# Attention transposes one tile later, and key copies by DMA, in a fused attention and linear-attention block

## The chip, the cores and the metric

The kernel runs on one core of one Trainium2 chip. The metric is the device time of one execution in microseconds (us), the median over several runs. A core has five engines with queues of their own: PE (TensorE: matmuls, with the weight loads shown as PEld), DVE (VectorE), ACT (ScalarE), POOL (GpSimd) and SP (SyncE), which here issues nearly all DMAs. Each engine works through its own list of instructions in order, and waits on semaphores for the others.

## The reference

One encoder layer on 512 positions of width 2048, in float32:

```
h    = rms_norm(x) * (1 + scale) + shift          # scale, shift, gate from silu(c) @ w_cond + b_cond
proj = h @ w_in                                   # queries, keys, values, gates, GLA inputs
for each of 3 (window, dilation) patterns:        # 16 heads x 64
    s = q k^T / 8 + bias, masked;  p = exp(s - max) / sum;  o = p v
att  = the three o, merged with weights from their softmax denominators
a_out = att * silu(ag)
g_out = rms_norm(gla_fwd + gla_bwd) * gain * silu(gg)   # 4 heads, chunked gated linear attention
x    = x + gate * (concat(a_out, g_out) @ w_out);  return rms_norm(x) * final_gain
```

The kernel folds the three patterns into one softmax per head, with the multiplicity of a key in the bias row.

## The kernel before

**Precision.** Matmul operands are split into a high part (rounded to the fast float32 form, `F32R`) and a low part (the rest); `three` (L168 to L171) multiplies high by high, low by high and high by low into one PSUM tile.

**Stages.** A planned start (conditioning sums, norm, values and the first projections, tiles `sta` and `stb`) runs until about 193 us. Then come *units*: one unit is one projection of 512 columns over all 2048 inputs, 64 steps ("ticks") of three 512-wide matmuls each, into four PSUM tiles. The units are `qk2`, `qk4`, `qk6`, `gk`, `gv0`, `gv1`, `ag0`, `ag1`, `gg0`, `gg1` and the output's `o0` to `o3`. A unit's weights come in eight groups of 512 KB (`raw_...`, `fetch`), fetched some groups ahead through four buffers and split by ACT (L313) and DVE (L297).

**Side work.** `unit` takes a list of side items, each with a place between 0 and 1, and issues each between ticks. Attention is the side work of `qk2`, `qk4`, `qk6` and `gk`: four heads in each, four query tiles of 128 per head, so 16 tiles a unit. `attention` builds 40 items, spread over the unit by `ATT_AT`:

- *score* (s): two matmuls (L576, L577) into PSUM tile `s`; DVE adds the bias row `g` and takes the extreme (L580), ACT takes the exponential with its sum (L583), DVE the reciprocal (L584), POOL scales the tile `p` by it (L585). `p` is a buffer of pool `t2`.
- *turn* (t): four PE transposes of `p` (L597) into PSUM tile `t`; ACT copies the high part (L601), DVE makes the low part (L602), both into `pt`.
- *values* (o): for two query tiles at once eight matmuls (L611) into `o`, then ACT (L614) and DVE (L618) into `cat`.

The items go out in the order s(x), t(x-1), o(x-2), where o comes only behind odd tiles. The first two items are moved to the unit's places 0.14 and 0.15, the last one over the unit's end. PSUM tiles `s`, `t` and `o` share three buffers (`PA`); the projections have five (`PJ`), of which a unit uses four.

**Stacks.** `qk_evict` takes the queries and keys of a pair of heads out of PSUM (at the end of the planned start, and at the end of each of the three `qk` units, so that it runs beside the start of the next one). A head's own 64 rows are one half of a 128-row tile. `qs` holds the queries' high part in the own half and the low part in the other; `ks` holds the keys' high part in *both* halves, `kl` the keys' low part in both. ACT writes the two halves of `ks` (L548, L549), DVE the two of `kl` (L550, L551), all read from PSUM. All twelve stack tiles of a unit and the `p` tiles are buffers of `t2`, 15 of 2 KB per partition.

**Order.** PE's order is that of the program. On the other engines a scheduler orders the instructions; `urgent` raises the priority of side items. In the stage in question every DMA goes out on SP.

Of the kernel before, what the change touches and what calls it, by code (L numbers as in the profile page):

```python
# [10 lines left out]
F32 = mybir.dt.float32  # L11
F32R = mybir.dt.float32r
I32 = mybir.dt.int32
AF = mybir.ActivationFunctionType
ALU = mybir.AluOpType
# [118 lines left out]
def block_kernel(ctx: ExitStack, tc: tile.TileContext, a: dict):  # L134
    nc = tc.nc
# [1 line left out]
    hp = ctx.enter_context(tc.tile_pool(name="hp", bufs=2))  # L137
    wp = ctx.enter_context(tc.tile_pool(name="wp", bufs=3))
    b8 = ctx.enter_context(tc.tile_pool(name="b8", bufs=8))
    t2 = ctx.enter_context(tc.tile_pool(name="t2", bufs=15))  # L140
    gp = ctx.enter_context(tc.tile_pool(name="gp", bufs=2))
    sm = ctx.enter_context(tc.tile_pool(name="sm", bufs=4))
    pp = ctx.enter_context(tc.tile_pool(name="pp", bufs=4, space=PSUM))
# [3 lines left out]
    def T2(name, dt=F32, parts=P):  # L147
        return t2.tile([parts, 512], dt, tag="t2", name=name)

    def B8(name, shape, dt=F32):  # L150
        return b8.tile([P] + shape, dt, tag="b8", name=name)
# [4 lines left out]
    def PA(name):  # L156
        return pp.tile([P, 512], F32, tag="pa", bufs=3, name=name)

    mm = nc.tensor.matmul
    tt = nc.vector.tensor_tensor  # L160
    stt = nc.vector.scalar_tensor_tensor
    act = nc.scalar.activation
# [314 lines left out]
    n = len(chain) // 2  # L477
# [53 lines left out]
    def qk_evict(p, psq, psk):  # L531

        for j in range(2):
            own = slice(64 * j, 64 * j + 64)
            oth = slice(64 - 64 * j, 128 - 64 * j)
            qs = T2(f"qs{p}{j}", F32R)
            act(qs[own], psq[own, ::-1], AF.Copy, scale=-0.125)
            stt(qs[oth], psq[own, ::-1], -0.125, qs[own].bitcast(F32),  # L540
                op0=ALU.mult, op1=ALU.subtract)
            stacks[2 * p + j] = [qs, None, None, own]
        for j in range(2):
            own = slice(64 * j, 64 * j + 64)
            oth = slice(64 - 64 * j, 128 - 64 * j)
            ks = T2(f"ks{p}{j}", F32R)
            kl = T2(f"kl{p}{j}", F32R)
            act(ks[own], psk[own], AF.Copy)  # L548
            act(ks[oth], psk[own], AF.Copy)  # L549
            tt(kl[own], psk[own], ks[own].bitcast(F32), op=ALU.subtract)  # L550
            tt(kl[oth], psk[own], ks[own].bitcast(F32), op=ALU.subtract)  # L551
            stacks[2 * p + j][1:3] = ks, kl

    cat = [None] * 4
# [1 line left out]
    def attention(pairs):  # L556

        tiles = [(2 * p + j, i) for p in pairs for j in range(2) for i in range(4)]
        gt, pt, pr_ = {}, {}, {}
        heads = [2 * p + j for p in pairs for j in range(2)]  # L560

        def g_load(h):
            g = gp.tile([P, 896], F32, tag="g", name=f"g{h}")
            nc.sync.dma_start(g, bass.AP(grow.tensor, grow.offset + h * 1024, [[1, P], [1, 896]]))
            gt[h] = g

        def score(h, i):
            def go():
                if h % 8 == 0 and i == 0:
                    cat[h // 8] = B8(f"cat{h // 8}", [4, 512])  # L570
                if i == 1 and h != heads[-1]:
                    g_load(h + 1)
                qs, ks, kl, _ = stacks[h]
                q = slice(P * i, P * i + P)
                ps = PA(f"s{h}{i}")
                mm(ps, qs[:, q], ks, start=True, stop=False)  # L576
                mm(ps, qs[:, q], kl, start=False, stop=True)  # L577
                t = T2(f"p{h}{i}")
                st = sm.tile([P, 3], F32, tag="st", name=f"st{h}{i}", bufs=6)
                nc.vector.tensor_tensor_reduce(  # L580
                    out=t, in0=ps, in1=gt[h][:, P * i:P * i + 512], op0=ALU.add, op1=ALU.min,
                    scale=1.0, scalar=3e38, accum_out=st[:, 0:1])
                act(t, t, AF.Exp, bias=st[:, 0:1], scale=-1.0, accum_out=st[:, 1:2])  # L583
                nc.vector.reciprocal(st[:, 2:3], st[:, 1:2])  # L584
                nc.gpsimd.tensor_scalar(t, t, st[:, 2:3], 1.0, op0=ALU.mult, op1=ALU.mult)  # L585
                pr_[h, i] = t
            return go

        def turn(h, i):
            def go():  # L590
                half, ii = divmod(i, 2)
                if ii == 0:
                    pt[h, half] = B8(f"pt{h}{half}", [2, 4, 256], F32R)
                t = pr_.pop((h, i))
                pk = PA(f"t{h}{i}")
                for kt in range(4):
                    nc.tensor.transpose(pk[:, kt * P:kt * P + P], t[:, kt * P:kt * P + P], ident)  # L597
                hi = pt[h, half][:, 0, :, P * ii:P * ii + P]
                lo = pt[h, half][:, 1, :, P * ii:P * ii + P]
                src = pk.rearrange("p (k q) -> p k q", k=4)  # L600
                act(hi, src, AF.Copy)  # L601
                tt(lo, src, hi.bitcast(F32), op=ALU.subtract)  # L602
            return go

        def values(h, half):
            def go():
                t = pt.pop((h, half))
                po = PA(f"o{h}{half}")
                for kt in range(4):
                    for w in range(2):  # L610
                        mm(po[:, :256], vv[h // 4][:, kt, h % 4, :], t[:, w, kt, :],  # L611
                           start=kt == 0 and w == 0, stop=kt == 3 and w == 1)
                oh = sm.tile([64, 256], F32, tag="oh", name=f"oh{h}{half}", bufs=1)
                act(oh, po[64:128, :256], AF.Copy)  # L614
                own = stacks[h][3]
                p = h // 2
                dst = cat[p // 4][own, p % 4, 256 - 256 * half:512 - 256 * half]
                tt(dst[:, ::-1], po[0:64, :256], oh, op=ALU.add)  # L618
            return go

        items = []
        n = len(tiles)
        for x in range(n + 3):
            if x < n:
                items.append(score(*tiles[x]))
            if 1 <= x <= n:
                items.append(turn(*tiles[x - 1]))
            if 2 <= x <= n + 1 and tiles[x - 2][1] % 2 == 1:
                items.append(values(tiles[x - 2][0], tiles[x - 2][1] // 2))
        g_load(heads[0])  # L630
        start, span, move0, move1, move_last = ATT_AT
        at = [start + (q + 0.5) / len(items) * span for q in range(len(items))]
        at[0] -= move0
        at[1] -= move1
        at[-1] += move_last
        return list(zip(at, items))
# [263 lines left out]
    for p in range(2):  # L900
        qk_evict(p, psb["b", 4 + 2 * p], psb["b", 5 + 2 * p])
    for n, p in (("qk2", 0), ("qk4", 2), ("qk6", 4)):
        ps = unit(n, False, attention((p, p + 1)) + ([(0.05, shift_row)] + some_sums(n) if p == 4 else []))
        for q in range(2):
            qk_evict(p + 2 + q, ps[2 * q], ps[2 * q + 1])

    ps = unit("gk", False, attention((6, 7)) + some_sums("gk"))
    gla["k"] = B8("gkt", [4, 512])
    for i in range(4):
# [221 lines left out]
```

## Time and profile before

| | |
|---|---|
| median of 3 runs | 975.26 us (973.75 to 977.06) |
| the profiled execution | 973.38 us, its span 971.6 us |
| PE busy | 943.0 us (97% of the span) |
| DVE, ACT, POOL busy | 616.6 (63%), 441.0 (45%), 81.6 us (8%) |
| chain that ended last | PE 81%, DVE 8%, DMA 3%, ACT 3%, issue 3% |
| DMA moved | 159.56 MB |
| granted TensorE clock | 0.997 of full |

Engine shares are of the whole span; the four units with attention fill about 193 to 476 us of it. The ends of matmuls are modelled: back-to-back 512-wide matmuls are listed with 0.39 us each, but start 0.23 us apart.

### The profile page before, as it was taken

What the parts mean: (1) busy time and instruction counts of PE and PEld (TensorE: products, weight loads), DVE (VectorE), ACT (ScalarE), POOL (GpSimd) and SP (SyncE); (2) the same over time, 40 slices, a digit from 0 to 9 for tenths busy, and PEclk for the clock granted to TensorE, in tenths of its full rate; (3) what the DMA queues carried; (4) which work ended last, traced back from release to release, by engine and by line L of the source; (5) the groups of instructions that cost most, each with busy time, mean ns of one, the idle gap of its engine ahead of it and who ended that gap; (6) DMA issues with size and microseconds to landing.
All of it is one profiled execution on the core that took longest, in us unless ns stands there. A gap on an engine that the chain in (4) does not pass through costs nothing.

```text
span 971.6 us, 11885 instructions
## 1 busy us (share of the span) xinstructions
PE 943.0 (97%) x4464; PEld 775.7 (80%) x4464; DVE 616.6 (63%) x916; ACT 441.0 (45%) x735; POOL 81.6 (8%) x100
## 2 busy tenths in 40 slices
PE   8999999989999999999999999999999999999996
PEld 4888788878778777778777888888888888888884
DVE  7988999566665676775534647585885352546431
ACT  5443533655655645655413544363744151333222
POOL 0000000011111122012000000000010000202120
PEclk9999999999999999999999999999999999999998
DMA  9998687422222253332444334355465455244013
GB/s 333 414 411 347 238 302 258 133 85 96 92 84 82 85 193 105 126 128 84 146 152 166 121 109 152 130 176 171 139 228 176 152 175 193 87 148 156 22 50 124
DMA packets 42619, 159.56 MB, mean 164 GB/s; under 512 B 5217, under 2 KB 5505, under 8 KB 37825
## 3 DMA queue, kind: packets, MB, share of 16 engines
q1 hardware_dynamic: 42386, 158.48, 47.2%
q8 instruction: 35, 0.57, 0.2%
q10 hardware_dynamic: 176, 0.33, 0.1%
q14 instruction: 22, 0.18, 0.1%
HBM read 154.51 MB, written 4.28 MB: 163 GB/s over the span
## 4 chain that ended last, share of the span: by engine, by line
PE 81%; DVE 8%; DMA 3%; ACT 3%; issue 3%; POOL 1%; SPq 0%; ACTq 0%; DVEq 0%; POOLq 0%
PE ps_o L170 6%; PE ps_o L171 6%; PE ps_o L169 6%; PE sta L169 3%; PE sta L170 3%; PE sta L171 3%; PE stb L171 3%; PE stb L169 3%; PE stb L170 3%; PE ps_qk L169 3%; PE ps_gv L170 3%; PE ps_gv L171 3%; PE ps_gv L169 3%; PE ps_qk L171 3%; PE ps_qk L170 3%
## 5 line engine op out<-in xcount | busy, mean ns | idle before, releaser
L585 POOL TENSOR_SCALAR p<-p,st 128x512 f32<-128x512 f32 x64 | 46.1, 721 | 424.3 <-DVE st L584 407.8
L583 ACT ACTIVATE p<-p,st 128x512 f32<-128x512 f32 x64 | 46.2, 722 | 63.4 <-DVE st L580 63.4
L244 DVE CUSTOM_DVE_ANT_0 cb<-cb,sb,c_bcond 128x2048 f32<-128x2048 f32 (+1 forms) x32 | 73.4, 2294 | 0.0
L602 DVE TENSOR_TENSOR pt<-t,pt 128x512 fp32r<-128x512 f32 x64 | 44.1, 689 | 17.8 <-ACT pt L601 17.8
L597 PE MATMUL t<-c_ident,p 128*128 128x128 f32 x256 | 38.9, 275 | 10.6 <-POOL p L585 10.6
L597 PEld LDWEIGHTS t<-c_ident,p 128*128 128x128 f32 x256 | 30.9, 140 | 22.3 <-POOL p L585 15.4
L580 DVE CUSTOM_DVE_ANT_0 p<-s,g 128x512 f32<-128x512 f32 x64 | 43.6, 686 | 7.0 <-PE s L577 6.1
L601 ACT ACTIVATE pt<-t 128x512 fp32r<-128x512 f32 x64 | 37.8, 591 | 21.1 <-PE t L597 20.5
L244 DVE CUSTOM_DVE_ANT_0 rawg<-rawg,sb,gate 128x1024 f32<-128x1024 f32 x16 | 20.7, 1294 | 27.8 <-DMA rawg<-in_wg 27.8
L611 PEld LDWEIGHTS o<-pt,vv 128*128 128x128 f32 x256 | 34.2, 189 | 3.8 <-DVE pt L602 1.7
L244 DVE CUSTOM_DVE_ANT_0 rawg<-rawg,sb,c_bcond 128x1024 f32<-128x1024 f32 x16 | 20.5, 1283 | 25.2 <-DMA rawg<-in_wg 25.2
L611 PE MATMUL o<-pt,vv 128*128 128x256 f32 x256 | 35.9, 283 | 0.0
L1014 POOL TENSOR_TENSOR x<-x,fgain 128x512 f32<-128x512 f32 x12 | 20.0, 1675 | 183.8 <-ACT ysq L1012 183.8
L1012 ACT ACTIVATE ysq<-x 128x512 f32<-128x512 f32 x16 | 10.1, 632 | 47.1 <-DVE x L1010 44.8
L767 POOL TENSOR_SCALAR dc<-st,sc 128x256 f32<-128x256 f32 x16 | 10.5, 656 | 242.5 <-DVE st L764 237.6
L584 DVE RECIPROCAL st<-st 128x1 f32<-128x1 f32 x64 | 10.4, 162 | 31.3 <-ACT p L583 31.2
L1009 DVE TENSOR_TENSOR y<-ps_o,sb 128x512 f32<-128x512 f32 x16 | 10.9, 684 | 25.9 <-PE ps_o L171 25.9
L576 PE MATMUL s<-ks,qs 128*128 128x512 f32 x64 | 25.3, 395 | 0.2 <-DVE qs L540 0.2
L577 PE MATMUL s<-kl,qs 128*128 128x512 f32 x64 | 25.0, 391 | 0.0
L774 ACT ACTIVATE sq<-st,sc 128x256 f32<-128x256 f32 x24 | 12.2, 509 | 26.2 <-DVE st L769 13.8
L618 DVE TENSOR_TENSOR cat<-o,oh 64x256 f32<-64x256 f32 x32 | 13.3, 415 | 11.9 <-ACT oh L614 11.7
L614 ACT ACTIVATE oh<-o 64x256 f32<-64x256 f32 x32 | 12.2, 380 | 17.3 <-PE o L611 16.5
(1279 smaller groups left out, 2944.6 us busy)
## 6 DMA issues: line engine op xcount, KB each, us to landing
cb<-in_wm SPq DMA_DIRECT2D x31, 1024.0 KB, 7.5
rawg<-in_wg SPq DMA_DIRECT2D x32, 512.0 KB, 3.4
raw_o<-in_w_o SPq DMA_DIRECT2D x32, 512.0 KB, 3.4
raw_qk<-in_w_qk SPq DMA_DIRECT2D x24, 512.0 KB, 3.3
rawb<-in_w_sb SPq DMA_DIRECT2D x16, 512.0 KB, 4.3
rawv<-in_wv SPq DMA_DIRECT2D x16, 512.0 KB, 3.4
raw_gv<-in_w_gv SPq DMA_DIRECT2D x16, 512.0 KB, 3.4
raw_ag<-in_w_ag SPq DMA_DIRECT2D x16, 512.0 KB, 3.4
```

The costliest lines, as they stand in the source:

```text
L169: mm(ps, lh, rh, start=first, stop=False)
L170: mm(ps, ll, rh, start=False, stop=False)
L171: mm(ps, lh, rl, start=False, stop=last)
L244: nc.vector.tensor_tensor_reduce(out=w, in0=w, in1=with_, op0=ALU.mult, op1=ALU.add, scale=1.0, scalar=init, accum_out=dst)
L576: mm(ps, qs[:, q], ks, start=True, stop=False)
L580: nc.vector.tensor_tensor_reduce(out=t, in0=ps, in1=gt[h][:, P * i:P * i + 512], op0=ALU.add, op1=ALU.min, scale=1.0, scalar=3e38, accum_o ...
L583: act(t, t, AF.Exp, bias=st[:, 0:1], scale=-1.0, accum_out=st[:, 1:2])
L585: nc.gpsimd.tensor_scalar(t, t, st[:, 2:3], 1.0, op0=ALU.mult, op1=ALU.mult)
L597: nc.tensor.transpose(pk[:, kt * P:kt * P + P], t[:, kt * P:kt * P + P], ident)
L601: act(hi, src, AF.Copy)
L602: tt(lo, src, hi.bitcast(F32), op=ALU.subtract)
L611: mm(po[:, :256], vv[h // 4][:, kt, h % 4, :], t[:, w, kt, :], start=kt == 0 and w == 0, stop=kt == 3 and w == 1)
```

## The change

1. The items of an attention unit go out in the order s(x), t(x-2), o(x-3): the transposes of a tile's P stand two score tiles behind its score matmuls, not one. The number of items and their places in the unit stay.
2. The second halves of `ks` and `kl` are copied out of the first halves by two DMAs on SP, 64 partitions x 2 KB (128 KB) each, in place of an ACT and a DVE instruction that read PSUM.
3. Pool `t2` has 16 buffers instead of 15; the 2 KB per partition come from a scratch area of another kind of DMA, which the kernel does not use.

```diff
-    t2 = ctx.enter_context(tc.tile_pool(name="t2", bufs=15))
+    t2 = ctx.enter_context(tc.tile_pool(name="t2", bufs=16))
...
             act(ks[own], psk[own], AF.Copy)
-            act(ks[oth], psk[own], AF.Copy)
+            nc.sync.dma_start(ks[oth].bitcast(F32), ks[own].bitcast(F32))
             tt(kl[own], psk[own], ks[own].bitcast(F32), op=ALU.subtract)
-            tt(kl[oth], psk[own], ks[own].bitcast(F32), op=ALU.subtract)
+            nc.sync.dma_start(kl[oth].bitcast(F32), kl[own].bitcast(F32))
...
-        for x in range(n + 3):
+        for x in range(n + 4):
             if x < n:
                 items.append(score(*tiles[x]))
-            if 1 <= x <= n:
-                items.append(turn(*tiles[x - 1]))
-            if 2 <= x <= n + 1 and tiles[x - 2][1] % 2 == 1:
-                items.append(values(tiles[x - 2][0], tiles[x - 2][1] // 2))
+            if 2 <= x <= n + 1:
+                items.append(turn(*tiles[x - 2]))
+            if 3 <= x <= n + 2 and tiles[x - 3][1] % 2 == 1:
+                items.append(values(tiles[x - 3][0], tiles[x - 3][1] // 2))
...
-                     dynamic_dma_scratch_size=4096)
+                     dynamic_dma_scratch_size=2048)
```

On PE, at the start of unit `qk2` (`s_` and `t_` are the PSUM tiles of a score and of transposes, `p_1553` the first tile's P, `ps_qk` the projection):

```order
 L171 MATMUL ps_qk_3_1512<-h_lo,qk21h 128x512
-L597 MATMUL t_1590<-c_ident,p_1553 128x128 x4
+L576 MATMUL s_1589<-ks_1477,qs_1471 128x512
+L577 MATMUL s_1589<-kl_1478,qs_1471 128x512
 L169 MATMUL ps_qk_3_1512<-h_hi,qk21h 128x512
 L170 MATMUL ps_qk_3_1512<-h_hi,qk21l 128x512
 L171 MATMUL ps_qk_3_1512<-h_lo,qk21h 128x512
-L576 MATMUL s_1600<-ks_1477,qs_1471 128x512
-L577 MATMUL s_1600<-kl_1478,qs_1471 128x512
+L597 MATMUL t_1602<-c_ident,p_1553 128x128 x4
```

The third score has taken the place of the first transposes, which now follow it one item later.

On DVE, the end of the stacks of the first four heads and the first score's work (`kl_` are key low parts, `qk23l` the low part of weights, `p_1553` the first tile):

```order
 L550 TENSOR_TENSOR kl_1484<-stb_882,ks_1483 64x512
-L551 TENSOR_TENSOR kl_1484<-stb_882,ks_1483 64x512
 L540 SCALAR_TENSOR_TENSOR qs_1489<-stb_887,qs_1489 64x512
 L540 SCALAR_TENSOR_TENSOR qs_1492<-stb_887,qs_1492 64x512
 L550 TENSOR_TENSOR kl_1496<-stb_894,ks_1495 64x512
-L551 TENSOR_TENSOR kl_1496<-stb_894,ks_1495 64x512
 L297 TENSOR_TENSOR qk23l<-raw_qk_1515,qk23h 128x1024
 L550 TENSOR_TENSOR kl_1502<-stb_894,ks_1501 64x512
-L551 TENSOR_TENSOR kl_1502<-stb_894,ks_1501 64x512
 L580 ISA p_1553,st_1554<-s_1550,g_1507 128x512
```

DVE has one instruction less per head ahead of the first score's work.

On SP, the same place (`raw_qk` are weight groups, `g` bias rows):

```order
 L286 DMA raw_qk_1612<-in_w_qk 128x1024
-L286 DMA raw_qk_1694<-in_w_qk 128x1024
-L286 DMA raw_qk_1788<-in_w_qk 128x1024
-L286 DMA raw_qk_1877<-in_w_qk 128x1024
-L564 DMA g_1699<-grow 128x896
+L549 DMA ks_1477<-ks_1477 64x512
+L551 DMA kl_1478<-kl_1478 64x512
+L549 DMA ks_1483<-ks_1483 64x512
+L286 DMA raw_qk_1698<-in_w_qk 128x1024
+L551 DMA kl_1484<-kl_1484 64x512
+L549 DMA ks_1495<-ks_1495 64x512
+L551 DMA kl_1496<-kl_1496 64x512
```

The copies stand among the weight loads, and SP waits at each for the first half to be written.

## The prediction

> **What bounds the kernel now.** I read the page's engine shares first, then the waits of PE, then PE's busy time by stage, then single places in the order of time.
>
> ```profile
> span 971.6 us, 11885 instructions
> PE 943.0 (97%) x4464; PEld 775.7 (80%) x4464; DVE 616.6 (63%) x916; ACT 441.0 (45%) x735; POOL 81.6 (8%) x100
> ```
>
> PE is the bound and has 28.6 us without work; DVE and ACT have room. So only PE's idle time can be won, and the waits say where it lies (us in total, times, longest):
>
> ```profile
> PE t L597 <- POOL p L585: 10.6, 11, 3.0
> PE pc L238 <- ACT c L236: 3.3, 1, 3.3
> PE ps_qk L169 <- DVE qs L540: 1.0, 2, 0.5
> ...
> PE ps_gk L169 <- DVE qs L540: 0.5, 1, 0.5
> ...
> PE ps_qk L169 <- DVE kl L551: 0.2, 1, 0.2
> PE ps_gk L169 <- DVE kl L551: 0.2, 1, 0.2
> PE s L576 <- DVE qs L540: 0.2, 1, 0.2
> ```
>
> The transposes' wait for P is 10.6 us; a new unit's wait for the old unit's PSUM tiles to be emptied into stacks is 1.9 us (1.0 + 0.5 + 0.2 + 0.2), with 0.2 us more at the first unit's second score. The 3.3 us belong to the start. By stage (span and PE busy are the first two numbers):
>
> ```profile
> 193.00:264.00 71.00, 67.38 (x356) 55.97 (x355) 46.41 (x95) 41.94 (x79) 11.08 (x16) 1.00 0.27 86
> 264.00:335.00 71.00, 68.98 (x362) 56.68 (x360) 46.31 (x96) 40.88 (x79) 11.10 (x16) 1.00 0.27 88
> 335.00:406.00 71.00, 67.16 (x351) 55.19 (x352) 50.50 (x104) 39.98 (x77) 12.84 (x16) 1.00 0.43 143
> 406.00:476.00 70.00, 66.65 (x350) 54.67 (x349) 46.53 (x97) 38.31 (x74) 11.09 (x16) 1.00 0.34 108
> ...
> 740.00:840.00 100.00, 100.00 (x443) 82.74 (x442) 44.94 (x51) 36.62 (x49) 6.88 (x4) 1.00 0.46 154
> ```
>
> The four attention units lose 3.6, 2.0, 3.8 and 3.4 us, 12.8 in all, which the waits above (12.7) nearly account for. Later units are full, so what is won here stays won. The granted clock is 1.00 throughout.
>
> **What a wait costs.** The first transposes of unit `qk2`:
>
> ```profile
> 203.35 0.39 PE L170 MATMUL ps_qk<-h_hi,qk21l 128*128 128x512 f32 x1
> 203.58 0.39 PE L171 MATMUL ps_qk<-h_lo,qk21h 128*128 128x512 f32 x1
> 207.00 0.66 PE L597 MATMUL t<-c_ident,p 128*128 128x128 f32 x4 [3.04 <-POOL p L585]
> ```
>
> Matmuls start 0.23 us apart (203.58 less 203.35) but are listed with 0.39, so a wait hides 0.16 us more than it shows. There are 11 + 2 + 1 + 1 + 1 + 1 = 17 such waits: 12.7 + 17 x 0.16 = 15.4 us is the most that can be won.
>
> **The transposes one tile later.** Nothing is added on PE: as many scores, transposes and values as before. Only the distance from a score to its transposes grows, by one tile's period, about 71 / 16 = 4.4 us in the middle of a unit (some 0.8 x 4.4 = 3.5, since the items fill 0.8 of it), and at the start and end of a unit by one item. Items stand 0.8 x 64 / 40 = 1.28 ticks apart, that is 1.28 x 3 x 0.23 = 0.88 us of projection.
>
> *First transposes of a unit.* Why P is late there:
>
> ```profile
> 202.90 0.69 DVE L550 TENSOR_TENSOR kl<-stb,ks 64x512 fp32r<-64x512 f32 x1
> 203.61 0.69 DVE L551 TENSOR_TENSOR kl<-stb,ks 64x512 fp32r<-64x512 f32 x1
> 204.33 0.69 DVE L580 CUSTOM_DVE_ANT_0 p<-s,g 128x512 f32<-128x512 f32 x1
> ...
> 206.26 1.38 POOL L585 TENSOR_SCALAR p<-p,st 128x512 f32<-128x512 f32 x2 [205.82 <-DVE st L584]
> ```
>
> PE had made that score by 199.0 (its first matmul, quoted further down, starts at 198.35, the second 0.23 later and lasts 0.39), but DVE was making stacks until 204.30. From the score's DVE step to P is 206.26 + 0.69 - 204.33 = 2.6 us. With four of DVE's stack instructions gone ahead of it (4 x 0.7 = 2.8 us) the step starts at about 201.5 and P is ready at about 204.1. The transposes are due one score (0.45) and one place (0.68 to 0.88) after 203.8 (203.58 + 0.23), at about 205.0. The 3.04 us go, with 0.8 to spare. The same in the other units:
>
> ```profile
> 270.13 0.39 PE L576 MATMUL s<-ks,qs 128*128 128x512 f32 x1
> ...
> 272.00 0.69 DVE L550 TENSOR_TENSOR kl<-ps_qk,ks 64x512 fp32r<-64x512 f32 x1
> 272.71 0.69 DVE L551 TENSOR_TENSOR kl<-ps_qk,ks 64x512 fp32r<-64x512 f32 x1
> 273.44 0.69 DVE L580 CUSTOM_DVE_ANT_0 p<-s,g 128x512 f32<-128x512 f32 x1
> ...
> 276.10 0.66 PE L597 MATMUL t<-c_ident,p 128*128 128x128 f32 x4 [0.81 <-POOL p L585]
> ```
>
> Here at least the last 1.4 us of stack work go (the weight split before it waits for ACT), and the transposes are due 1.1 later: 2.5 us against a wait of 0.8, also in the third and fourth unit (0.8 each). Together 3.04 + 3 x 0.8 + 4 x 0.16 = 6.1 us.
>
> *Inside the units with conditioning sums.* The longest such wait:
>
> ```profile
> 362.80 1.28 DVE L244 CUSTOM_DVE_ANT_0 rawv<-rawv,shb,vbias 128x1024 f32<-128x1024 f32 x1 [1.68 <-DMA rawv<-in_wv]
> 364.01 0.69 DVE L580 CUSTOM_DVE_ANT_0 p<-s,g 128x512 f32<-128x512 f32 x1
> ...
> 366.90 0.66 PE L597 MATMUL t<-c_ident,p 128*128 128x128 f32 x4 [1.99 <-POOL p L585]
> ```
>
> DVE stood at a sum whose operand was still loading, with the score behind it. Such a hold of 1.68 + 1.28 us will come again, but 3.5 us more of distance cover the 1.99 us that were left. The units' last transposes waited too. With the first unit's 3.04 and the three 0.8 taken off the 10.6, both kinds are 5.2 us in 7 waits: 5.2 + 7 x 0.16 = 6.3. For what an in-order DVE still holds up I keep back 1.0. The bounds are 0 and the 1.68 + 1.28 in full in each of the two units with sums, 5.9; it stands nearer to 0, because the distance gained is more than such a hold.
>
> *What comes late next.* At a unit's end two transposes now follow each other and then o: from the last-but-two transposes to the o that needs both is two items instead of three. What o needs behind transposes (ACT's copy, then DVE's):
>
> ```profile
> 207.70 0.60 ACT L601 ACTIVATE pt<-t 128x512 fp32r<-128x512 f32 x1 [1.12 <-PE t L597]
> ...
> 208.33 0.69 DVE L602 TENSOR_TENSOR pt<-t,pt 128x512 fp32r<-128x512 f32 x1 [1.55 <-ACT pt L601]
> ```
>
> That is 209.02 - 207.00 = 2.0 us, against two items, 2 x 0.88 + 0.45 = 2.2, with ACT and DVE busy splitting weights there. I take 0.2 us in each of four units, 0.8 (0 to 0.69, one DVE step, each).
>
> **The copies by DMA.** They remove 16 instructions each from ACT and DVE (12 from the `qk` units, 4 from the start's PSUM tiles):
>
> ```profile
> L549 ACT ACTIVATE ks<-ps_qk x12: 588/592/597, 259.3 to 412.2; 64x512 fp32r<-64x512 f32 x12
> ...
> L551 DVE TENSOR_TENSOR kl<-ps_qk,ks x12: 683/688/694, 261.3 to 413.5; 64x512 fp32r<-64x512 f32 x12
> ```
>
> That is 9.5 us of ACT and 11.0 of DVE, off the bound but in the way of PSUM tiles. In a new unit PE waits 0.50 us for the second pair's queries; ahead of these DVE loses two and ACT two instructions, over 1.2 us, so the waits of 1.9 + 0.2 us go: 2.1 + 6 x 0.16 = 3.1.
>
> The trace shows no copy from SBUF to SBUF. Its landing is bounded by transfers on the same queue in the same stage (min/median/max; srow 8 KB, raw_qk 512 KB, g 448 KB):
>
> ```profile
> DMA to landing us min/median/max: 1.3/1.3/1.3
> ...
> DMA to landing us min/median/max: 3.1/3.3/4.5
> ...
> DMA to landing us min/median/max: 3.2/4.0/5.8
> ```
>
> The tightest consumer is the first score of `qk2`:
>
> ```profile
> 193.57 0.68 DVE L550 TENSOR_TENSOR kl<-stb,ks 64x512 fp32r<-64x512 f32 x1 [0.52 <-ACT ks L549]
> ...
> 198.35 0.39 PE L576 MATMUL s<-ks,qs 128*128 128x512 f32 x1
> ```
>
> From 194.25 to 198.35 there are 4.1 us; I take 3 (128 KB lies between 8 and 512): no wait; at 5.8, 1.7 us. In the later units DVE began the second half at 261.3 at the earliest (the L551 row), when the first was done, and the score came at 270.13: 8.8 us.
>
> The Trainium skill ("SBUF — State Buffer", the section on the DMA setup-cost knee) speaks against small transfers: a fixed 2 us plus the bytes at 436 GB/s, so by its figures a copy would take an estimated 2.3 us. By that rule the sum has nothing for the copies; by the slowest row above it has 1.7 us. No run here shows the fixed part for such a copy.
>
> SP waits at each copy for ACT or DVE with weight loads queued behind it, some 8 us over a boundary. The loads are early: the group that ACT reads at 226.34 was issued at 196.24.
>
> ```profile
> 196.24 0.33 SPq L286 DMA_DIRECT2D raw_qk<-in_w_qk  x1
> ...
> 226.34 1.06 ACT L313 ACTIVATE qk26h<-raw_qk 128x1024 fp32r<-128x1024 f32 x1 [0.80 <-PE ps_qk L171]
> ```
>
> ACT waited for PE to free a buffer there, not for the load: nothing. The load of the row that the sums need (`shb`) now stands behind the last `kl` copy of its boundary; DVE makes that one's first half ahead of a weight split that it followed before, so it is ready by then: nothing. The sixteenth `t2` buffer holds the third live P: nothing, since otherwise DVE would wait for it.
>
> **The sum.** 6.1 + 6.3 + 3.1 = 15.4 us, less 1.0 and 0.8: 13.6. From the profiled execution, whose span of 971.6 is 973.4 with what lies around it, that makes 959.8; from the median shown, 1.9 higher, 961.7. I forecast 961 us. Its own range goes from 15.4 won off 973.4 (958) to 10 off the median (965).
>
> **Rivals.**
>
> *Half.* The hold on DVE and ACT is not one of a few us: with the scheduler's order ACT copies two tiles' transposes before the third exponential, and with sums behind loads most mid-unit and end waits (5.3 of the 6.3 less 1.0) and some 1.5 elsewhere stay: 13.6 - 5.3 - 1.5 = 6.8 won, 968 (961 + 6.8). Against it: DVE is busy 46 to 51 of 71 us, so a queue drains within a tile's period. Chance 0.13.
>
> *It does not do what it says.* P comes as much later as its transposes do, because the engines do other work first; only the unit starts gain, 3.1: 971, or none: 975. For it: the order puts a weight split ahead of the first score's step. Chance 0.05.
>
> *Slower: the copies land late.* The first score of every unit then waits for its copies, PE with it. The units give 4.1, 8.8, 8.8 and 8.8 us, so a landing of L us costs 4L - 30.5. It eats the 14 us between 961 and the median at L = 11.2 and ends 3 us slower, at 978, at L = 11.9. Against it: 5.8 is the longest in this stage, at a DMA share of 0.27 to 0.43. Chance 0.04.
>
> **Chances.** 0.78 for the forecast. About 0.3% (3 us) is what a measurement of this kernel can tell from no change. Faster: 0.78 + 0.13 = 0.91; same 0.05; slower 0.04. The range from 957 (all 15.4 off the profiled execution, and a us more) to 968.5 takes in the half case.
>
> **What would show it.** After the change the waits of transposes for P should fall from 10.6 to about 1 us, those of projections for `qs` and `kl` to nothing; PE's idle time in the four units from 12.8 to 2 us; the first score's DVE step of `qk2` should start some 2.5 us after PE made it, not 5.4. New rows to look for: o waiting for `pt`, s waiting for a DMA of `ks` or `kl`, and landing of the copies near 3 us. Wrong if P's wait keeps more than 4 us, or if a stage after 476 us, full now, shows idle PE.

## The result and the profile after

The changed kernel takes 958.34 us (median, 957.66 to 959.90), the kernel before 974.50 in the runs beside it: a ratio of 0.9839, 95% interval 0.9823 to 0.9855. The profiled execution took 959.90 us, its span 957.9. The forecast was 961.

The page's first lines after the change:

```profile
span 957.9 us, 11999 instructions
PE 939.7 (98%) x4464; PEld 777.1 (81%) x4464; DVE 605.3 (63%) x900; ACT 431.5 (45%) x719; POOL 81.1 (8%) x100
```

The span is 13.7 us shorter: PE has 18.2 us without work instead of 28.6, and is listed as busy for 3.3 us less, since a wait hides a part of itself behind the modelled end of the matmul before it. ACT and DVE have 16 instructions less each. PE's waits (us in total, times, longest):

```profile
PE pc L238 <- ACT c L236: 3.4, 1, 3.4
PE gn L819 <- ACT gsh L817: 1.2, 1, 1.2
PE go L805 <- DVE at L791: 1.0, 1, 1.0
PE o L611 <- DVE pt L602: 0.8, 1, 0.8
```

No transposes wait for P, and no projection for `qs` or `kl`: all of the 12.7 us are gone. New are one wait of o for `pt` and two in later units (`go` and `gn`, matmuls of the linear attention), which come and go between executions. The stage is best measured by where it begins and ends on PE, the first matmul of `qk2` and the first of `gv0`. Before:

```profile
192.23 0.39 PE L169 MATMUL ps_qk<-h_hi,qk20h 128*128 128x512 f32 x1
...
473.51 0.39 PE L169 MATMUL ps_gv<-gv00h,h_hi 128*128 128x512 f32 x1
```

After:

```profile
191.87 0.39 PE L169 MATMUL ps_qk<-h_hi,qk20h 128*128 128x512 f32 x1
...
457.51 0.39 PE L169 MATMUL ps_gv<-gv00h,h_hi 128*128 128x512 f32 x1
```

The four units took 281.3 us (473.51 - 192.23) and take 265.6 (457.51 - 191.87): 15.6 us less. By unit they are full now, except the last (span and PE busy first):

```profile
191.80:257.20 65.40, 65.37 (x345) 54.89 (x345) 43.40 (x90) 38.88 (x75) 11.15 (x16) 1.00 0.37 112
257.20:323.60 66.40, 66.37 (x354) 55.89 (x353) 41.93 (x89) 37.41 (x73) 11.17 (x16) 1.00 0.36 108
323.60:390.20 66.60, 66.57 (x355) 55.91 (x354) 47.24 (x100) 37.62 (x74) 11.13 (x16) 1.00 0.52 163
390.20:457.40 67.20, 66.36 (x354) 55.89 (x353) 44.98 (x94) 36.53 (x71) 12.05 (x16) 1.00 0.42 132
```

The start of `qk2` on DVE and PE, which the prediction walked through:

```profile
199.91 0.69 DVE L550 TENSOR_TENSOR kl<-stb,ks 64x512 fp32r<-64x512 f32 x1
200.63 0.69 DVE L580 CUSTOM_DVE_ANT_0 p<-s,g 128x512 f32<-128x512 f32 x1
```

```profile
197.99 0.39 PE L576 MATMUL s<-ks,qs 128*128 128x512 f32 x1
...
202.97 0.39 PE L576 MATMUL s<-ks,qs 128*128 128x512 f32 x1
204.11 0.60 PE L597 MATMUL t<-c_ident,p 128*128 128x128 f32 x4
```

The first score's DVE step starts 2.0 us after PE ends that score (198.6), against 5.4 before, and the transposes follow the third score without a wait.

The copies land in 2.2 us, the keys' low parts in 2.4 (KB each, us from issue to landing):

```profile
ks<-ks SPq DMA_DIRECT2D x16, 128.0 KB, 2.2
kl<-kl SPq DMA_DIRECT2D x16, 128.0 KB, 2.4
```

### The profile page after: what moved, and what is told of

Same layout as the page of the kernel before. It is cut to its first block, busy times and chain, and to the rows that moved or that the text cites. A ratio compares the mean times of both kernels' runs of the same rounds, so it can differ in the third digit from the quotient of the medians.

```text
span 957.9 us, 11999 instructions
## 1 busy us (share of the span) xinstructions
PE 939.7 (98%) x4464; PEld 777.1 (81%) x4464; DVE 605.3 (63%) x900; ACT 431.5 (45%) x719; POOL 81.1 (8%) x100
## 4 chain that ended last, share of the span: by engine, by line
PE 84%; DMA 6%; DVE 5%; issue 3%; ACT 1%; SPq 0%; POOL 0%; ACTq 0%; DVEq 0%; POOLq 0%
PE ps_o L170 6%; PE ps_o L169 6%; PE ps_o L171 6%; DMA rawg<-in_wg 6%; PE ps_qk L170 5%; PE ps_qk L169 5%; PE ps_qk L171 5%; PE o L611 3%; PE sta L169 3%; PE sta L170 3%; PE sta L171 3%; PE stb L171 3%; PE stb L169 3%; PE stb L170 3%; PE ps_gv L171 3%; PE ps_gv L170 3%
## 5 line engine op out<-in xcount | busy, mean ns | idle before, releaser
L602 DVE TENSOR_TENSOR pt<-t,pt 128x512 fp32r<-128x512 f32 x64 | 44.0, 689 | 16.2 <-ACT pt L601 15.8
L1009 DVE TENSOR_TENSOR y<-ps_o,sb 128x512 f32<-128x512 f32 x16 | 10.9, 684 | 25.9 <-PE ps_o L171 25.9
L1010 DVE TENSOR_TENSOR x<-y,x 128x512 f32<-128x512 f32 x16 | 18.0, 1125 | 0.3
```

## The experiments

The length of the four attention units is taken as above, from one profile of each kernel; the kernel before and the changed one, each profiled twice, agree with themselves within 0.1 us there. Ratios are to the kernel before, on the same chip. The medians come from three chips and are compared by their ratios, or where two kernels ran on one chip. In summary:

| kernel | tiles behind | copies | four units, us | median, us | ratio (95% interval) |
|---|---|---|---|---|---|
| before, second profile | 1 | ACT, DVE | 281.2 | 972.33 (one run) | |
| lag only | 2 | ACT, DVE | 272.8 | 963.48 | 0.9892 (0.9874 to 0.9910) |
| copies only | 1 | DMA | 271.4 | 964.29 | 0.9894 (0.9879 to 0.9910) |
| after, again | 2 | DMA | 265.6 | 957.30 | 0.9809 (0.9788 to 0.9830) |
| 15 buffers | 2 | DMA | 265.6 | 958.74 | 0.9837 (0.9820 to 0.9854) |
| copies twice | 2 | DMA x2 | 266.4 | 958.13 | 0.9834 (0.9816 to 0.9851) |
| copies four times | 2 | DMA x4 | 283.9 | 976.92 | 1.0012 (0.9997 to 1.0028) |
| lag three | 3 | DMA | 263.7 | 955.36 | 0.9788 (0.9766 to 0.9809) |
| lag three only | 3 | ACT, DVE | 268.6 | 961.24 | 0.9855 (0.9829 to 0.9881) |
| fifth raw buffer | 2 | DMA | 265.9 | 959.22 | 0.9829 (0.9807 to 0.9851) |

**The order alone.** Against the changed kernel:

```diff
-            nc.sync.dma_start(ks[oth].bitcast(F32), ks[own].bitcast(F32))
+            act(ks[oth], psk[own], AF.Copy)
...
-            nc.sync.dma_start(kl[oth].bitcast(F32), kl[own].bitcast(F32))
+            tt(kl[oth], psk[own], ks[own].bitcast(F32), op=ALU.subtract)
```

> The order s(x), t(x-2), o(x-3) and 16 buffers, but the second halves of ks and kl made by ACT and DVE as before. My theory (three terms, each with its own part of the change): the waits inside the units and at their ends go by the distance alone (6.3 less 1.8), the first transposes of units 2 to 4 too (2.9), of the first unit's 3.2 us only the 1.1 by which the transposes are due later; the waits of projections for qs and kl (1.9 us, 3.1 with what they hide) stay. Sum 8.5 won: about 966 us, P's wait about 2 us, all in the first unit. Rival, the distance is all: 958 us, as with the whole change, and no wait for qs or kl either. Rival, the freed ACT and DVE are all: 974 us.

**The copies alone.** Against the kernel before:

```diff
-            act(ks[oth], psk[own], AF.Copy)
+            nc.sync.dma_start(ks[oth].bitcast(F32), ks[own].bitcast(F32))
...
-            tt(kl[oth], psk[own], ks[own].bitcast(F32), op=ALU.subtract)
+            nc.sync.dma_start(kl[oth].bitcast(F32), kl[own].bitcast(F32))
```

> The old order s(x), t(x-1), o(x-2), but the copies by DMA and 16 buffers. My theory: the unit starts win their 3.1 us, and the first score's DVE step comes 2.8 us sooner in the first unit and 1.4 in the others, which takes 2.8 and 2.9 us from the first transposes' waits; the waits inside and at the ends of units (5.2 listed) stay. Sum 8.8 won: about 966 us, P's wait 5 to 5.5 us. With the kernel with the order alone this adds up to more than the whole change, since both take the first transposes' wait (4 us). Rival, the distance is all: 974 us. Rival, the freed engines are all: 958 us.

PE's waits with the order alone:

```profile
PE t L597 <- POOL p L585: 2.0, 2, 1.3
...
PE ps_qk L169 <- DVE qs L540: 1.0, 2, 0.6
PE o L611 <- DVE pt L602: 0.8, 1, 0.8
PE ps_gk L169 <- DVE kl L551: 0.8, 1, 0.8
...
PE ps_gk L169 <- DVE qs L540: 0.5, 1, 0.5
PE s L576 <- DVE kl L551: 0.5, 1, 0.5
```

and with the copies alone, where none is left for `qs` or `kl`:

```profile
PE t L597 <- POOL p L585: 5.4, 7, 1.4
```

The order alone wins 8.5 us in the units, as expected to the tenth, and keeps 2.0 us of waiting for P; but only 1.3 of these stand in the first unit, 0.7 at the start of the fourth. The agreement to the tenth is partly luck: o behind `pt` costs more than was kept back for it (2.0 us, see below), a score now waits 0.5 us for `kl`, and the 1.0 us kept back for DVE was not needed. The copies alone win 9.8 (8.8 expected) and keep 5.4 us of waiting for P (5 to 5.5 expected), all inside units and at their ends. Together that is 18.3, and the whole change has 15.6. Of the 2.7 us between them the first transposes' waits are the main part, since those go by either; read from the matmuls' starts they alone would make about 3.5, and waits that are new in one of the two kernels (the score's for `kl` with the order alone, one of 1.35 us for P in `qk6` with the copies alone) take some back. The rivals of both runs fall. In the medians the two win 11.7 and 10.9 us, in the other order than in the units; each is more than its units show, so a us or two of a median belongs to the spread of the other stages.

**Fifteen buffers.** `bufs=15` in place of 16 for `t2`, and the scratch area as before; each engine's list is word for word that of the changed kernel.

> The whole change with 15 buffers in t2 instead of 16; every engine's order is that of the changed kernel. The prediction said that without the sixteenth buffer DVE would wait for one. By that, the score's DVE step waits at each unit's start until the transposes two tiles back are done, up to one tile's period (3.5 us) in each of four units, of which the distance hides most: 959 to 964 us. Rival: a third live P is free before the fourth score is made, because its transposes stand ahead of that score on PE: no wait, 958 us within 1.

The units take 265.6 us, to 0.02 as with sixteen. The rival holds: the sixteenth buffer does nothing.

**Copies twice and four times.** Each of the two lines of copies stands two or four times.

> The whole change, with each of the 32 copies made twice to the same place; the second waits on SP for the first to land, and the score waits for the second. So a copy counts as landed some 2.5 to 5 us later and SP is held up four times as long at each boundary. My theory, copies and queue are covered: the first unit's cover (4.1 us from the first half of kl to the score, 2.2 used by the landing) is used up, 0 to 1.5 us there, none in the other units, and weights come early enough: 958 to 960 us. Rival, the cover is about as long as the landing: all four units wait, 962 us or more, with rows of s waiting for a DMA. Rival, the weights behind the copies are the limit: ACT waits for raw_qk, 962 us or more.

> The whole change, with each copy made four times to the same place, each waiting on SP for the one before. Twice cost 0.4 us in each of two units. My theory: a copy counts as landed some 7 us later than once and more with the others' on SP between; the first unit's cover (2.2 us beyond one landing) is gone by 5 us or more and PE waits there for the DMA of kl; the other units (6 us beyond one landing) lose 0 to 4; weights behind the copies come later too. 965 to 985 us, with rows of s waiting for a DMA, or of ACT waiting for raw_qk. Rival, SP and the DMA are never the limit in this stage: 958 to 960 us.

Twice costs 0.7 us in the units and nothing in the median: 0.4 in `qk2`, where the first score's weight load waits 0.5 us for the copy of `kl`, and 0.4 in `qk6`, where none was expected and a score's weight load waits for DVE's `pt`, not for a copy. Four times costs 18.3 us in the units (7.2, 1.5, 3.2 and 6.4 in order; 0 to 4 were expected in the later ones) and the whole win:

```profile
PE s L582 <- DMA ks<-ks: 7.3, 2, 4.2
...
PE s L583 <- DMA kl<-kl: 2.1, 3, 0.8
```

Its longest wait is that of the first score of `qk2`:

```profile
202.66 0.77 PE L582 MATMUL s<-ks,qs 128*128 128x512 f32 x1 [4.21 <-DMA ks<-ks]
```

So the mechanism of the prediction's slower rival exists, beyond a cover that two copies in a row nearly fit into (the cover is the time from the first half's end to the first matmul that needs the copy). The two waits listed make 9.4 of the 18.3 us. With the two longest (4.2 us, and 3.1 in `gk`) PE also ran slower: the granted clock was 0.55 from 202 to 208 us and 0.57 from 412 to 420, and some 20 matmuls there started about 0.43 us apart instead of 0.23, an estimated 4 us in all. Behind the 3.0 us wait of the kernel before it was 1.00 (207 to 212 us). None of PE's waits in these units is for weights, so SP's hold on the weight loads is not seen to cost anything even here. Of the remaining 5 us, 1.3 are o behind `pt`; the rest, smaller delays for the most part at late scores, was not taken apart further.

**Three tiles behind.** Against the changed kernel:

```diff
-        for x in range(n + 4):
+        for x in range(n + 5):
...
-            if 2 <= x <= n + 1:
-                items.append(turn(*tiles[x - 2]))
-            if 3 <= x <= n + 2 and tiles[x - 3][1] % 2 == 1:
-                items.append(values(tiles[x - 3][0], tiles[x - 3][1] // 2))
+            if 3 <= x <= n + 2:
+                items.append(turn(*tiles[x - 3]))
+            if 4 <= x <= n + 3 and tiles[x - 4][1] % 2 == 1:
+                items.append(values(tiles[x - 4][0], tiles[x - 4][1] // 2))
```

> The whole change with the transposes three score tiles behind, not two. My theory: with two, no transposes wait for P any more, so a third tile's distance has nothing to take away: the four attention units keep their 265.6 us within 1, 957 to 960 us. Rival, the last wait of the stage (o for pt, 0.84 us) is also one of distance: 0.8 us less. Rival, four live P's in sixteen buffers hold up DVE at a unit's start: some 1 to 3 us more, with DVE waiting ahead of the score's step.

My theory was wrong here: the units get another 2.0 us shorter (0.3, 0.3, 0.3 and 1.1 in order), and this is the fastest kernel of all, 955.36 us (954.38 to 955.78) against 957.30 (956.99 to 957.69) on the same chip. Where the 2.0 us were is seen in the weight loads' waits between 185 and 470 us; after the change they are

```profile
PEld o L611 <- DVE pt L602: 2.2, 4, 1.2
PEld plr L924 <- issue: 0.8, 1, 0.8
```

and with three tiles behind only the second row is left. The four waits are one near each unit's end, where the o of two tiles follows the second one's transposes too closely. PE's own list has only the longest of them (0.8 us); by the starts of o's matmuls the four cost 2.0 us, and with three tiles behind nothing.

**Three tiles behind, without the copies.** Both edits above.

> Transposes three score tiles behind, second halves of ks and kl by ACT and DVE as before the change, 16 buffers. With two tiles behind and no copies the units took 272.8 us, with P's wait at 2.0, those for qs and kl at 2.8 and o's for pt at its part. My theory: more distance takes P's 2.0 (2.3 with what it hides) and o's 2.0, not the waits of a new unit for qs and kl nor of the first score, which only fewer instructions on ACT and DVE shorten: 268 to 269 us in the units, 958 to 960 us. Rival, distance alone does it all: 264 us in the units, 955 us, and the copies are not needed.

268.6 us, as my theory had it; the waits for `qs` and `kl` stay (the median is 1 us above its range). Distance alone does not replace the copies: they are worth 5.0 us (268.6 - 263.7) even then.

**The later units.** In the first profile after the change `ag1` and `gg0` took 112.0 us, 2.4 more than in the profile before. Three kernels ask about that.

> The kernel before, once more, for a second profile. The medians fell by some 16 to 18 us, the four attention units by 15.6 in the profiles. My theory: the attention units take 281.3 us again, to 0.1, and the rest of the difference is spread of the other stages (ag1 and gg0, and the start), in which executions of one kernel differ by 1 to 3 us. Rival: the units themselves vary in the kernel before (more waits for P), 282 us or more in this execution.

> The changed kernel itself once more, beside the others on one chip, for its spread and a second profile. My theory: the four attention units take 265.6 us again, to 0.1, since orders and durations there repeat; ag1 and gg0 do not repeat (111.98 us in the first profile; the same orders gave 108.9 and 109.0 in two other kernels) and come out between 108.5 and 112. Rival, the change itself costs 2.4 us there: 112 us again.

> The whole change with 15 buffers in t2 and a fifth buffer for weights and sums (raw), for which the scratch area gives up the rest. My theory: the sixteenth t2 buffer does nothing, and what the units ag1 and gg0 lose in some executions (2.4 us in the profile after the change, 0 to 1 in others) is DVE standing at a gate sum whose operand is still loading; a fifth buffer starts such loads one sum earlier: DVE's waits for rawg fall by half or more, ag1 and gg0 together come to 108.5 us, 956 to 958 us. Rival, the loads are late because the queue is busy, not for want of a buffer: the waits for rawg stay, 958 to 959 us.

The kernel before repeats its units (281.2 us) and takes 109.0 us for `ag1` and `gg0` (109.6 in the first profile); the changed kernel repeats its units (265.6) and takes 109.0 there, without the 2.4. So that loss is spread of single executions, not the change's: seven other profiles, with one edit or another, have 108.5 to 110.4 us there. DVE's waits for the gate sums' operands, with four `raw` buffers (the changed kernel again) and with five:

```profile
DVE rawg L244 <- DMA rawg<-in_wg: 51.0, 23, 4.5
```

```profile
DVE rawg L244 <- DMA rawg<-in_wg: 29.4, 17, 4.7
```

They fell by 42%, not by the half expected, but `ag1` and `gg0` took 110.5 us instead of 108.5 and the median is 1.9 us above that of the changed kernel beside it: neither the theory nor its rival came out. The fifth buffer changes the orders of DVE, ACT and SP too, and PE waited 1.0 us for a state (`att` for `st`; 0.2 to 0.4 in the first two profiles). What sets those two units' spread stays open.

## Why the prediction was right

*The bound and where the win lies.* Right: all of the 15.6 us came from PE's waits in the four units, and nothing that was full before changed its length beyond the spread (161.2 us from `gv0` to `ag1` and 227.2 from `gg1` to the end, before and after).

*The transposes' waits.* Right in kind and close in size: 6.1 us were put on the first transposes and 6.3, less 1.0 kept back, on the others. All went, so the 1.0 was not needed. The distance covers the holds on DVE: they are still there (its waits for `rawv` in the second half of the stage), but nothing on PE follows from them.

*What comes late next.* The right place, o behind `pt` at a unit's end, but mis-sized: 0.8 us were taken, and it costs 2.0 (265.64 less 263.66 with three tiles behind), 1.1 of it in the last unit:

```profile
449.51 1.22 DVE L297 TENSOR_TENSOR gv01l<-raw_gv,gv01h 128x1024 fp32r<-128x1024 f32 x1
...
450.72 1.27 DVE L244 CUSTOM_DVE_ANT_0 rawv<-rawv,shb,vbias 128x1024 f32<-128x1024 f32 x1
...
451.91 1.29 DVE L602 TENSOR_TENSOR pt<-t,pt 128x512 fp32r<-128x512 f32 x2
```

```profile
452.65 1.10 PE L611 MATMUL o<-pt,vv 128*128 128x256 f32 x7 [0.84 <-DVE pt L602]
```

A weight split and a conditioning sum stand on DVE ahead of the two `pt` steps there, and ACT's two copies for the neighbouring transposes come one behind the other; the prediction priced only the chain of a single tile.

*The most that can be won.* Wrong: 15.4 us was said to be the upper end, and three tiles behind win 17.6 (281.28 less 263.66). The sum took PE's listed waits and 0.16 us more for each. Comparing the starts of the matmuls, kind by kind, in the kernel before and with three tiles behind puts 12.9 us on the transposes (12.4 in the sum, 10.6 + 11 x 0.16), 3.3 on the projections (2.7 in the sum), 0.6 on the scores (0.4 in the sum), and 0.4 each on o and behind one `pshift` matmul, two places that the sum had at nothing. So a wait hides some 0.2 us rather than 0.16, as the matmuls after it start late too, and small delays that PE's list does not show were left out. The weight loads of the kernel before list waits for o as well:

```profile
PEld o L611 <- DVE pt L602: 1.7, 8, 0.3
```

Most of that was hidden from PE: o's matmuls started only 0.4 us late in all.

*The copies.* Right: 3.1 us at the unit starts were forecast, and the copies alone have no wait left there. A landing of 3 us was taken; 2.2 and 2.4 were measured (medians; the slowest took 4.3), where the Trainium skill's fit ("SBUF — State Buffer", the section on the DMA setup-cost knee) gives an estimated 2.3. The trace agrees with that estimate, which was nearer than the 3 us taken. It tests the fit's fixed 2 us and hardly its rate: the bytes make only an estimated 0.3 us of it, at a rate that the section gives for all 16 ports, while the copies span 64 partitions.

*Weights, `shb` and SP.* Right: none of the waits listed ahead of the steps that read `raw_qk` ends on a load (for 3.8 us of them the profile names no releaser), and the units are full. The cover in the first unit was sized about right: 4.1 us were taken, and after the change it is 4.8, from 193.40, where DVE ends the first half of `kl`, to 198.21, where the matmul that reads it starts. Two landings in a row overrun it by 0.4 us.

*The sixteenth buffer.* The cost, nothing, was right; the reason given (otherwise DVE would wait) was wrong, as fifteen show.

*The numbers.* 13.6 us were forecast; 15.6 came in the units and 16.2 in the medians. Three misses partly cancel: the upper end was 2.2 too low, the 1.0 kept back for DVE was not needed, and o cost 1.2 more than the 0.8 kept back for it, which gives 13.6 + 2.2 + 1.0 - 1.2 = 15.6. That the total came so near owes something to luck; the waits named and the way they go were right. None of the rivals came about.

## What to carry to other kernels

Where an in-order engine is the bound and side work reaches it through three other engines, put more items between producer and consumer before shortening the chain; then look for the consumer that now stands too close to its neighbour. Read the waits of the weight loads beside those of the matmuls: some stalls of PE show only there. What such a wait costs is read from the starts of the matmuls, since a part of it, or all, can be hidden. A copy made by DMA is free only up to a cover in time: work it out from the first half's end to the first use, and try it by making the copy twice.

## What the runs showed that I had not expected

SP takes 0.46 us to issue most copies between two halves of SBUF, and 0.33 for a load from HBM in the profile before. After the change:

```profile
193.43 0.46 SPq L551 DMA_DIRECT2D kl<-kl  x1
194.17 0.46 SPq L549 DMA_DIRECT2D ks<-ks  x1
194.81 0.46 SPq L286 DMA_DIRECT2D raw_qk<-in_w_qk  x1
```

The load between the copies takes 0.46 as well, and the last one ahead of the copies, at 188.97, took 0.33; so it is not the kind of transfer alone; what makes it so was not tried. And the two parts of the change, each near 1.1% alone, overlap by only 2.7 us of 18.3, although both shorten the same wait.
